# Seven-product (2x2 block) form for the u and output products of a gating layer, and a new pair order in the MLPs

## The chip, the cores and the metric

One core of one Trainium2 chip runs the whole program. The metric is the device time in microseconds (us) of one execution; the number quoted for a kernel is the median of a few runs.

## The reference, cut to what matters

The trunk has four residual layers over 1024 positions of width 1024: a spatial gating layer, an MLP, an RWKV-7 layer and another MLP. The gating layer and the MLPs are what the change touches.

```python
# gating layer: E = 2048, 16 groups of 128 channels, blocks of 128 positions
z = gelu(rmsnorm(x) @ w_in + b_in)            # 1024x1024 @ 1024x4096
u, v = split(z, 2)                            # 2048 columns each
v = layernorm(v) * ln_g + ln_b                # over the 2048 channels
s = einsum('gij,bnjgc->bnigc', w_s * mask, v) + b_s    # one 128x128 matrix for each group
x = x + (u * s) @ w_out                       # 1024x2048 @ 2048x1024
# MLP, after the gating layer and after the RWKV layer
x = x + square(relu(rmsnorm(x) @ w1)) @ w2    # 1024x1024 @ 1024x4096, 1024x4096 @ 4096x1024
```

## The kernel before, in words

Every fp32 product is done as three matmuls on a high and a low part of each operand (`mm3`, lines 155 to 159: high by high, low by high, high by low). The high part is a cast on ScalarE (ACT), the low part a subtraction on VectorE (DVE); `split` does both. One such matmul of 128 x 128 weights by 512 columns is one row of TensorE (PE).

**MLPs** (`mlp`). Both products of an MLP go by a 2x2 block scheme with seven block products instead of eight. `SIDES` names them: M1 = A11 B11, M2 = A12 B21, M3 = S4 B22, M4 = A22 T4, M5 = S1 T1, M6 = S2 T2, M7 = S3 T3, where the S are sums of blocks of the activations and the T sums of blocks of the weights. The first product ("up") runs over 16 pairs of hidden tiles; a product of a pair is 12 matmuls. `prepare(n)` makes the weights of the n-th product six products ahead: `load_pair` brings 2 x 512 KB of w1, `sums` makes T1 to T4 on GpSimd (POOL), `split` makes high and low part in a ring of six buffers. `evict` takes each PSUM result out, squares it, and forms S1 to S4 of the hidden values; all seven blocks are stored to DRAM (`zd`). `seq` is the order of the products: pair p's products are interleaved with M4 and M3 of pair p-1, and the result tiles (`y_of`) alternate between x0 to x3 and x4 to x7. The second product ("dn") has 28 steps (4 groups by 7 products) of 4 quarters, 12 matmuls each; a unit u is half a step's operands: `load_z` brings the stored blocks, `load_w` the tiles of w2, `prepare_z` and `prepare_w` split them (four operand tiles a unit), and `chain` multiplies and adds the result into the residual tiles `xd`. Unit u+4 is prepared while step n runs, u = 2n and 2n+1. The table `meanwhile` says after which of the last products of up the first loads and preparations of dn are issued; from product -14 on the order on PE, DVE, ACT and SyncE (SP, which issues the DMAs) is the written one (`manual_schedule`). Everywhere else a scheduler sets the order.

**Between the layers** `Spread` (before an MLP) takes each residual tile t, stores it (`xmf`), scales it by its norm (`scale`, into one of two tiles xn, here sn_f) and transposes it on PE (`transpose`, tiles st_f). From tiles 0 to 3 come A22 and S1, from tiles 4 to 7 A11, A12, S2, S3 and S4, all split into high and low. `transpose(t-1)` is called right after `scale(t)`.

**Gating layer** (`sgu`). First v in 8 column blocks c (1536 matmuls of 256 columns), kept in 8 SBUF tiles V, with gelu on ACT and the statistics of the layer norm on DVE. Then 16 groups g: two halves of u with 24 matmuls each (768 in all), gelu into x6 or x7, four mixing matmuls for each half into PSUM (s), a DVE operation for scale and bias (line 896, gt), and the product u*s on DVE (line 901). At every second group the v tile is normalised by eight DVE operations (line 877). Then the output product: 8 blocks c, each of 8 tiles t by 2 halves by 6 matmuls (768 in all), added to x on DVE (line 928); during c = 7, `Spread` runs for each finished tile.

**RWKV** (`rwkv`) ends in an output product `product(c, w, ts, out)` over four blocks c; in the last one, c = 3, `Spread` runs tile by tile.

## Time and profile before

| | us |
|---|---|
| median of 3 runs | 2748.62 (2747.3 to 2748.93) |
| the profiled execution, its own time | 2749.38 |
| its span, first to last instruction | 2747.7 |
| PE busy in the span | 2609.6 (95%) |
| DVE busy | 1885.7 (69%) |
| ACT busy | 968.8 (35%) |
| POOL busy | 624.3 (23%) |

The span is what the trace shows; 1.7 us of the execution lie around it. Times in the trace are counted from the span's start. In stages: v until 208 us, u and mixing until 414, the output product until about 595, the first MLP's up until about 922 and dn until 1249, RWKV until about 2093, the second MLP's up until about 2421 and dn to the end.

### The profile page before, as it was taken

Reading aid. Unit: us, or ns where it says so; the run is one execution under the profiler, and the core shown is the slowest. Engines: PE = TensorE matmul, PEld = TensorE weight load, DVE = VectorE, ACT = ScalarE, POOL = GpSimd, SP = SyncE. Lnnn points to the kernel's source line nnn. Section 1 sums busy time; section 2 is a strip of 40 time slices with the busy share of each in tenths; the row PEclk is TensorE's granted clock in tenths of the full one; section 3 lists DMA queues with packets and bytes.
Section 4 is the critical chain, followed back from the end, with each engine's and each line's share of the span. In section 5 each row is a group of like instructions: output and inputs, shape, how many; then the busy total and the mean of one; then the engine's idle time right before and its main releaser. Section 6 shows DMA issues by size and latency. Waiting matters only on the chain. (4 is left out here: it accounts for less than half of the span.)

```text
span 2747.7 us, 41554 instructions
## 1 busy us (share of the span) xinstructions
PE 2609.6 (95%) x16394; PEld 2206.3 (80%) x16394; DVE 1885.7 (69%) x2957; ACT 968.8 (35%) x1579; POOL 624.3 (23%) x481
## 2 busy tenths in 40 slices
PE   8999999989999999999999999977897999989998
PEld 8998888867888778877677898967776888878887
DVE  6446236787666687786667548999678756677777
ACT  4222111243333333345554332324414333333334
POOL 2000000044333000012465413244424333200002
PEclk9999999999999999999899999989899999999999
DMA  5111112124444744332576864444742444384432
GB/s 174 51 47 48 46 58 81 55 91 154 153 146 146 286 166 161 123 115 80 184 178 166 214 170 117 113 101 96 196 131 93 163 138 158 130 324 150 138 130 92
DMA packets 329076, 368.36 MB, mean 134 GB/s; under 512 B 89288, under 2 KB 241968, under 8 KB 328880
## 3 DMA queue, kind: packets, MB, share of 16 engines
q1 hardware_dynamic: 326672, 359.07, 42.0%
q0 software_dynamic: 2064, 6.36, 0.8%
q8 instruction: 129, 2.11, 0.3%
q14 instruction: 67, 0.55, 0.1%
q10 hardware_dynamic: 144, 0.26, 0.0%
HBM read 252.32 MB, written 113.31 MB: 133 GB/s over the span
## 5 line engine op out<-in xcount | busy, mean ns | idle before, releaser
L77 DVE TENSOR_TENSOR wls<-raw,whs 128x1024 fp32r<-128x1024 f32 x84 | 109.7, 1312 | 163.5 <-ACT whs L76 163.2
L76 ACT CAST whs<-raw 128x1024 fp32r<-128x1024 f32 x88 | 91.4, 1047 | 236.7 <-PE wo L159 73.8
L157 PE MATMUL v<-whs,ht_n 128*128 128x256 f32 x512 | 145.3, 284 | 0.2 <-ACT ht_n L307 0.2
L159 PE MATMUL v<-whs,ht_n 128*128 128x256 f32 x512 | 144.3, 282 | 0.2 <-DVE ht_n L162 0.2
L158 PE MATMUL v<-wls,ht_n 128*128 128x256 f32 x512 | 144.2, 282 | 0.0
L331 DVE TENSOR_TENSOR w1s<-w1r,w1s 128x512 fp32r<-128x512 f32 x96 | 90.6, 945 | 63.6 <-ACT w1s L335 63.6
L159 PE MATMUL dnu<-oph 128*128 128x512 f32 x336 | 132.1, 393 | 0.0
L157 PE MATMUL dnu<-oph 128*128 128x512 f32 x336 | 132.1, 393 | 0.0
L158 PE MATMUL dnu<-oph 128*128 128x512 f32 x336 | 131.5, 391 | 0.0
L331 DVE TENSOR_TENSOR xd<-xd,dnu 128x512 f32<-128x512 f32 x128 | 87.5, 684 | 58.4 <-PE dnu L159 58.2
L631 ACT CAST oph<-w2B 128x1024 fp32r<-128x1024 f32 x72 | 75.5, 1049 | 127.5 <-DVE w2B L331 127.5
L629 ACT CAST oph<-zr 128x1024 fp32r<-128x1024 f32 x72 | 75.4, 1048 | 112.4 <-issue 71.5
L928 DVE TENSOR_TENSOR x<-wo,x 128x512 f32<-128x512 f32 x112 | 75.6, 688 | 42.2 <-PE wo L159 42.1
L157 PE MATMUL p<-xs,whs 128*128 128x512 f32 x256 | 104.4, 408 | 0.1
L159 PE MATMUL upc<-sS_f,w1s 128*128 128x512 f32 x256 | 101.2, 395 | 2.8 <-DVE w1s L331 2.8
L158 PE MATMUL p<-xs,whs 128*128 128x512 f32 x256 | 102.3, 400 | 0.9 <-DVE xs L1025 0.9
L159 PE MATMUL p<-xs,wls 128*128 128x512 f32 x256 | 101.9, 399 | 1.1 <-DVE wls L77 1.1
L158 PE MATMUL upc<-sS_f,w1s 128*128 128x512 f32 x256 | 101.7, 397 | 0.8 <-POOL sS_f L331 0.8
L157 PE MATMUL u<-ht_n,whs 128*128 128x512 f32 x256 | 101.7, 397 | 0.0
L157 PE MATMUL upa<-sS_f,w1s 128*128 128x512 f32 x256 | 101.7, 397 | 0.0
L157 PE MATMUL upc<-sS_f,w1s 128*128 128x512 f32 x256 | 101.3, 396 | 0.3 <-ACT sS_f L363 0.3
L158 PE MATMUL upa<-sS_f,w1s 128*128 128x512 f32 x256 | 101.3, 396 | 0.0
(605 smaller groups left out, 8119.3 us busy)
## 6 DMA issues: line engine op xcount, KB each, us to landing
w1r<-in_ffn_w_dram SPq DMA_DIRECT2D x64, 512.0 KB, 4.1
w2B<-in_ffn_w_dram SPq DMA_DIRECT2D x64, 512.0 KB, 5.5
raw<-in_sgu_w_in_dram SPq DMA_DIRECT2D x32, 512.0 KB, 4.2
raw<-in_rwkv_w_rkv_dram SPq DMA_DIRECT2D x32, 512.0 KB, 4.6
...
```

Of the source, the lines that this page charges most:

```text
L76: nc.scalar.copy(out=wh, in_=raw)
L77: (low or nc.vector).tensor_tensor(out=wl, in0=raw, in1=wh.bitcast(F32), op=ALU.subtract)
L157: nc.tensor.matmul(o, sh, mh, start=first, stop=False, skip_group_check=more)
L158: nc.tensor.matmul(o, sh, ml, start=False, stop=False, skip_group_check=more)
L159: nc.tensor.matmul(o, sl, mh, start=False, stop=last, skip_group_check=more)
L331: eng.tensor_tensor(out=out, in0=x, in1=y, op=op)
L629: nc.scalar.copy(out=four[0], in_=z)
L631: nc.scalar.copy(out=four[2], in_=b)
L928: nc.vector.tensor_tensor(out=xs[t][:, dc], in0=o, in1=(xin[t] if c == 0 else xs[t])[:, dc], op=ALU.add)
```

## The change

The function `mlp` becomes `two_products(i, sides, w1, w2, residual, after_factory, gate=None)`, and the gating layer uses it too, with a `Gate`.

- **Gating, u**: 8 pairs of groups by 7 products by 12 matmuls. S1 to S4 of the layer's input are made during v's blocks c = 4 to 7 (`sums_of_halves`: 8 POOL operations, 3 casts on ACT and 3 low parts on DVE for each of four slices), S4's split after v.
- **Gating, v**: two SBUF tiles instead of eight; each finished half block goes to DRAM (`vd`, 16 stores). For each pair its v comes back into x4 to x7 in two loads and is normalised there, four operations on DVE and four on ACT. The mixing matrices and biases also go through DRAM and are reloaded for each pair.
- **Gating, output**: dn's code with 14 steps of 48 matmuls. The residual comes from the kernel's input x.
- **All three two-product stages**: one pair at a time, in the order M1, M5, M6, M2, M7, M3, M4; the MLPs still begin with M5 and M4 of pairs 0 and 1. The result tiles are x0 to x3 alone; x4 to x7 are free at the end of up. T3 and T4 are made on POOL with the product that needs them.
- **Up to dn**: a new table `meanwhile`. The loads of x4 to x7 and of units 0 to 3 come after product -14; the w2 loads after -7 and -4.
- **Spread**: three xn tiles; a tile's transposes come `lag` calls of `tick` after its scaling (3 before the first MLP, 5 before the second). In the gating layer it now runs in the last three steps of dn. In RWKV's output, blocks 2 and 3 of tiles 4 to 7 are interleaved, where block 2 stood ahead of block 3.

```diff
     def scale(self, t):
-        x, xn = self.xs[t], self.xns[t % 2]
+        x, xn = self.xs[t], self.xns[t % 3]
...
     def __call__(self, t):
         self.scale(t)
-        if t > 0:
-            self.transpose(t - 1)
-        if t == NT - 1:
-            self.transpose(t)
+        self.wait.append([t, 0])
...
+    def tick(self):
+        for w in self.wait:
+            w[1] += 1
+        if self.wait and self.wait[0][1] >= self.lag:
+            self.transpose(self.wait.pop(0)[0])
...
-    seq = [("M5", 0), ("M4", 0), ("M5", 1), ("M4", 1), ("M1", 0), ("M2", 0), ("M6", 0), ("M7", 0)]
-    for p in range(1, NP):
-        seq += [("M1", p), ("M4", p - 1), ("M2", p), ("M3", p - 1), ("M6", p), ("M5", p), ("M7", p)]
+    seq = [("M5", 0), ("M4", 0), ("M5", 1), ("M4", 1)] if early else []
+    for p in range(NP):
+        seq += [(m, p) for m in ("M1", "M5", "M6", "M2", "M7", "M3", "M4")]
...
-            ys[p] = [xt(4 * (p % 2) + j, f"y{j}{p}_{i}").rearrange("p (e n) -> p e n", e=2) for j in range(4)]
+            ys.extend(xt(j, f"y{j}_{i}").rearrange("p (e n) -> p e n", e=2) for j in range(4))
...
             elif m == "M6":
                 nc.scalar.copy(out=u2, in_=bank("a", p))
+                nc.scalar.copy(out=y2[:, 1], in_=bank("c", p))
+                if gate:
+                    gate.mix(p, "C11", s24[:, 0])
+                    gate.mix(p, "C12", s24[:, 1])
...
-    meanwhile = {
-        -14: [lambda: load_z(0), lambda: load_z(1)],
-        -8: [lambda: load_w(0, ("B11", "B12"))],
-        -7: [lambda: load_z(2), lambda: load_z(3), lambda: load_w(0, ("B22", "B21"))],
-        -6: [lambda: prepare_z(0), lambda: prepare_w(0)],
-        -5: [lambda: load_x(range(4, 8))],
-        -4: [lambda: prepare_z(1), lambda: prepare_w(1)],
-        -1: [lambda: load_w(1, ("B12", "B11")), lambda: load_x(range(4))],
-    }
...
+        meanwhile = {
+            -14: [lambda: load_x(range(4, 8))] + [lambda u=u: load_z(u) for u in range(4)],
+            -7: [lambda: load_w(0, ("B11", "B12"))],
+            -4: [lambda: load_w(0, ("B22", "B21")), lambda: unit(0)],
+            -3: [lambda: unit(1)],
+        }
...
         up(ready, len(seq))
-        for u in (2, 3):
-            prepare_z(u)
-            prepare_w(u)
+        for f in held:
+            f()
+        load_x(range(4))
+        load_w(1, ("B12", "B11"))
+        unit(2)
+        unit(3)
...
+        def mix(self, p, name, th):
+            e, hf = int(name[2]) - 1, 2 - int(name[1])
+            g = 2 * p + e
+            o = pt(f"s{p}{name}").rearrange("p (n i) -> p n i", n=4)
+            for n in range(4):
+                nc.tensor.matmul(o[:, n, :], self.v[p][hf][:, n, e * P : (e + 1) * P], self.ws[:, 0, e],
+                                 start=True, stop=True)
...
-    product(2, wo[2], range(4, NT), xz)
     xs = [xt(t, f"x2_{t}") for t in range(NT)]
     after = after_factory(xs)
-    product(3, wo[3], range(NT), xs)
+    tick.append(after.tick)
+    product(3, wo[3], range(4), xs)
+    for t in range(4, NT):
+        product(2, wo[2], [t], xz)
+        product(3, wo[3], [t], xs)
```

**Where instructions stand now.** First SP's queue at the end of the second MLP's up. zd1_7... <- y are the stores of the last pair, w2B the loads of w2, xd <- xmf the residual tiles, zr <- zd1_0S3 and zd1_1S3 units 6 and 7, the ones for M7, dn's fourth step. Before:

```order
L513 DMA zd1_7S3_18161<-y215_1_20356 128x512
L513 DMA zd1_7A12_18157<-y015_1_20354 128x512
L513 DMA zd1_7S4_18162<-y315_1_20357 128x512
L584 DMA w2B121_1_20488<-in_ffn_w2_dram 128x2x512 x2
L584 DMA w2B111_1_20491<-in_ffn_w2_dram 128x2x512 x2
L674 DMA xd0_1_18167<-xmf1_0_17685 128x1024
L674 DMA xd1_1_18168<-xmf1_1_17686 128x1024
L674 DMA xd2_1_18169<-xmf1_2_17687 128x1024
L674 DMA xd3_1_18170<-xmf1_3_17688 128x1024
L593 DMA zr1_1_20364<-zd1_0S3_18112 128x1024
L593 DMA zr1_1_20364<-zd1_1S3_18119 128x1024
L593 DMA zr0_1_20219<-zd1_0A22_18109 128x1024
```

Now:

```order
L522 DMA zd1_7S3_18246<-y2_1_18302 128x512
L522 DMA zd1_7S4_18247<-y3_1_18303 128x512
L737 DMA xd0_1_20536<-xmf1_0_17730 128x1024
L737 DMA xd1_1_20538<-xmf1_1_17731 128x1024
L737 DMA xd2_1_20540<-xmf1_2_17732 128x1024
L737 DMA xd3_1_20542<-xmf1_3_17733 128x1024
L639 DMA w2B121_1_20544<-in_ffn_w2_dram 128x2x512 x2
L639 DMA w2B111_1_20547<-in_ffn_w2_dram 128x2x512 x2
L645 DMA zr1_1_20277<-zd1_0S3_18197 128x1024
L645 DMA zr1_1_20277<-zd1_1S3_18204 128x1024
L645 DMA zr0_1_20274<-zd1_0A22_18194 128x1024
```

The loads of xd0 to xd3 stand ahead of the w2 loads where they stood behind them; those of xd4 to xd7, which stood among the last pair's stores, have gone some 60 rows up, to product -14, with the first four unit loads.

Second, PE at the join from RWKV to the second MLP: wo23 are matmuls of `product(3)`, st the transposes of `Spread`, upc0 and upd0 the first two products of up. Before:

```order
L159 MATMUL wo23_71_18037<-wsp6_17603,yh11_17402 128x512
L157 MATMUL wo23_71_18037<-wsp7_17606,yh10_17401 128x512
L158 MATMUL wo23_71_18037<-wsp7_17606,yh10_17401 128x512
L159 MATMUL wo23_71_18037<-wsp7_17606,yh11_17402 128x512
L383 MATMUL st40_f1_17943<-ident_76,sn4_f1_17681 128x128 x4
L383 MATMUL st41_f1_17948<-ident_76,sn4_f1_17681 128x128 x4
L157 MATMUL upc0_1_18212<-sS1_f1_17764,w1s0_1_18187 128x512
L157 MATMUL upd0_1_18228<-sA22_f1_17763,w1s1_1_18190 128x512
L158 MATMUL upd0_1_18228<-sA22_f1_17763,w1s1_1_18190 128x512
L158 MATMUL upc0_1_18212<-sS1_f1_17764,w1s0_1_18187 128x512
L159 MATMUL upc0_1_18212<-sS1_f1_17764,w1s0_1_18187 128x512
```

Now:

```order
L160 MATMUL wo22_71_18130<-wsp5wh_17403,yh10_17511 128x512
L161 MATMUL wo22_71_18130<-wsp5wl_17404,yh10_17511 128x512
L377 MATMUL st50_f1_18098<-ident_81,sn5_f1_17728 128x128 x4
L162 MATMUL wo22_71_18130<-wsp5wh_17403,yh11_17512 128x512
L160 MATMUL wo23_70_18138<-wsp6_17713,yh10_17511 128x512
L161 MATMUL wo23_70_18138<-wsp6_17713,yh10_17511 128x512
L162 MATMUL wo23_70_18138<-wsp6_17713,yh11_17512 128x512
L160 MATMUL wo23_70_18138<-wsp7_17716,yh10_17511 128x512
L161 MATMUL wo23_70_18138<-wsp7_17716,yh10_17511 128x512
L162 MATMUL wo23_70_18138<-wsp7_17716,yh11_17512 128x512
L160 MATMUL wo23_71_18146<-wsp6_17713,yh10_17511 128x512
```

The transposes of tile 4 stood behind the last matmul of the output product, and those of tiles 5 to 7 among the first products of up. Now those of tile 4 stand in the block ahead of this piece, those of the first half of tile 5 in it, and blocks 2 (wo22) and 3 (wo23) of tile 7 alternate.

Third, DVE in the gating layer: wls and w1s are low parts of weights, gt and s the mixing, y the result tiles, upb, upa and upc the PSUM results of the products. Before, two groups:

```order
L77 TENSOR_TENSOR wls33_3474<-raw33_3321,whs33_3473 128x1024
L896 SCALAR_TENSOR_TENSOR gt13_3458<-s13_0_3459,sguv_1060,bs1_114 128x512
L896 SCALAR_TENSOR_TENSOR gt13_3458<-s13_1_3466,sguv_1060,bs1_114 128x512
L901 TENSOR_TENSOR v6_1892<-gt13_3458,u13_3405 128x4x128 x2
L77 TENSOR_TENSOR wls34_3556<-raw34_3403,whs34_3555 128x1024
L896 SCALAR_TENSOR_TENSOR gt14_3540<-s14_0_3541,sguv_1060,bs1_114 128x512
L896 SCALAR_TENSOR_TENSOR gt14_3540<-s14_1_3548,sguv_1060,bs1_114 128x512
L901 TENSOR_TENSOR v7_2129<-gt14_3540,u14_3487 128x4x128 x2
```

Now, half of one pair:

```order
L1042 SCALAR_TENSOR_TENSOR y3_2_2557<-s2C11_2971,sguv_1070,ta_2_2495 128x512
L327 TENSOR_TENSOR w1s22_2_2983<-ta_2_2495,w1s22_2_2983 128x512
L1042 SCALAR_TENSOR_TENSOR y3_2_2557<-s2C12_2977,sguv_1070,ta_2_2495 128x512
L327 TENSOR_TENSOR y0_2_2554<-upb2_2_2986,tu_2_2558 128x512
L327 TENSOR_TENSOR w1s23_2_3001<-tb_2_2496,w1s23_2_3001 128x512
L1024 TENSOR_SCALAR vn41_3090<-vn41_3090,ri_v_2452,vnmr_2450 128x256 x2
L327 TENSOR_TENSOR y0_2_2554<-y0_2_2554,y3_2_2557 128x512
L327 TENSOR_TENSOR y1_2_2555<-y1_2_2555,upa2_2_2896 128x512
L327 TENSOR_TENSOR w1s24_2_3034<-w1r31_2_2773,w1s24_2_3034 128x512
L1042 SCALAR_TENSOR_TENSOR y2_2_2556<-s2C22_3018,sguv_1070,ta_2_2495 128x512
L1042 SCALAR_TENSOR_TENSOR y2_2_2556<-s2C21_3024,sguv_1070,ta_2_2495 128x512
L327 TENSOR_TENSOR y1_2_2555<-y1_2_2555,y2_2_2556 128x512
```

Where two groups held two low parts, four mixing operations (line 896) and four products (line 901), with the normalising of v at every second group, a pair now holds seven low parts, four mixing operations (line 1042), four normalisings (line 1024), three subtractions or additions that take a PSUM result out, four products and S1 to S4. The program has 11817 rows on PE before and 11629 now.

## Rows read from the trace of the kernel before

**Rows 1.** Windows: us, length, busy (count) of PE, PEld, DVE, ACT, POOL, clock, DMA share, GB/s.

```profile
208.00:414.30 206.30, 206.30 (x1027) 172.69 (x1025) 84.31 (x152) 43.41 (x55) 0.00 (x0) 1.00 0.18 54
414.30:576.00 161.70, 161.70 (x712) 133.34 (x712) 112.58 (x148) 29.84 (x28) 10.26 (x8) 1.00 0.21 72
...
628.00:916.00 288.00, 288.00 (x1245) 233.40 (x1245) 189.69 (x264) 95.00 (x164) 92.98 (x68) 1.00 0.46 157
```

**Rows 2.** Windows at the four joins and of their half-clock remainders.

```profile
573.00:626.00 53.00, 43.60 (x204) 33.01 (x203) 51.69 (x95) 33.12 (x65) 26.72 (x20) 0.94 0.21 81
609.90:617.30 7.40, 4.60 (x13) 3.57 (x13) 6.94 (x10) 2.75 (x5) 3.31 (x3) 0.54 0.00 0
...
965.20:968.80 3.60, 3.60 (x9) 2.83 (x10) 3.60 (x4) 0.99 (x2) 0.00 (x0) 0.50 0.59 233
...
2069.60:2114.10 44.50, 31.56 (x160) 24.48 (x160) 44.02 (x83) 25.03 (x51) 19.04 (x13) 0.98 0.24 93
2114.10:2122.50 8.40, 6.71 (x18) 4.54 (x19) 4.84 (x8) 3.93 (x7) 6.22 (x5) 0.50 0.02 6
...
2461.80:2467.30 5.50, 5.50 (x13) 4.34 (x14) 5.50 (x7) 2.89 (x4) 0.00 (x0) 0.51 0.51 180
```

**Rows 3.** PE's waits, gating to first MLP (570 to 640): total, times, longest.

```profile
PE st_f L383 <- DVE sA_f L331: 3.2, 2, 2.6
PE upc L159 <- DVE w1s L331: 2.8, 1, 2.8
```

**Rows 4.** PE's waits, RWKV to second MLP (2065 to 2125).

```profile
PE st_f L383 <- DVE sA_f L331: 8.8, 3, 6.4
PE st_f L383 <- DVE sn_f L374: 5.0, 3, 3.0
```

**Rows 5.** PE's waits from up to dn, first MLP (916 to 966), then second (2410 to 2470).

```profile
PE dnu L157 <- DVE xd L331: 9.1, 1, 9.1
PE upa L157 <- ACT u_f L538: 0.7, 1, 0.7
...
PE dnu L157 <- DVE xd L331: 7.3, 1, 7.3
```

**Rows 6.** Timeline of SP and ACT, second MLP, up to dn: start, length, instruction, [idle before].

```profile
2430.10 0.32 SPq L513 DMA_DIRECT2D zd_7S<-y  x1
2432.54 3.35 SPq L584 DMA_DIRECT2D w2B<-in_ffn_w_dram  x4
2437.30 1.76 SPq L674 DMA_DIRECT2D xd<-xmf  x4
2439.17 0.37 SPq L593 DMA_DIRECT2D zr<-zd_0S  x1
...
2449.50 1.05 ACT L629 CAST op6raw<-zr 128x1024 fp32r<-128x1024 f32 x1 [11.43 <-DMA zr<-zd_0S]
```

**Rows 7.** Groups by form, gating's u stage (210 to 414): count, busy us, mean ns, idle before.

```profile
L886 ACT ACTIVATE u<-u,sguv 128x512 f32<-128x512 f32 x32 | 21.9, 685 | 89.9 <-PE u L159 89.9
L896 DVE SCALAR_TENSOR_TENSOR gt<-s,sguv,bs 128x512 f32<-128x512 f32 x30 | 21.2, 744 | 1.0 <-PE s L893 0.9
L877 DVE TENSOR_SCALAR v<-v,ri_v,vnmr 128x256 f32<-128x256 f32 x64 | 21.1, 407 | 0.0
...
L901 DVE TENSOR_TENSOR v<-gt,u 128x512 f32<-128x512 f32 x30 | 19.4, 683 | 0.0
```

**Rows 8.** Groups by form in the first MLP's up (640 to 900).

```profile
L331 DVE TENSOR_TENSOR w1s<-w1r,w1s 128x512 fp32r<-128x512 f32 x41 | 39.1, 954 | 28.8 <-ACT w1s L335 28.8
...
L331 POOL TENSOR_TENSOR te<-tb,w1r 128x512 f32<-128x512 f32 x13 | 20.6, 1587 | 47.8 <-DVE w1s L331 47.8
...
L331 DVE TENSOR_TENSOR w1s<-ta,w1s 128x512 fp32r<-128x512 f32 x14 | 13.9, 992 | 0.0
...
L331 DVE TENSOR_TENSOR w1s<-te,w1s 128x512 fp32r<-128x512 f32 x13 | 8.8, 676 | 0.0
```

**Rows 9.** Groups by form in the first MLP's dn (969 to 1249), DVE.

```profile
L331 DVE TENSOR_TENSOR oph<-zr,oph 128x1024 fp32r<-128x1024 f32 x30 | 36.5, 1218 | 0.2 <-ACT oph L629 0.2
```

More of the change, by code (lines that the diff above doesn't have):

```diff
@@ L172, in trunk, with channel_vectors @@
     nc.gpsimd.memset(zero, 0.0)
-    def channel_vectors(name, parts):
+    def channel_vectors(name, parts, tag):
         n = sum(v.shape[0] // P for v in parts)
-        stage = zt(7, f"{name}_stage")[:, :P]
+        stage = tp.tile([P, HB], F32, tag=tag, name=f"{name}_stage")[:, :P]
         r = 0
@@ L522, in with_q21, with with_q12, finish, rest @@
             store(p, "S3", s13[:, 1])
-        sp0.u[1] = tp.tile([P, HB], F32, tag="td", name=f"u2_{i}")
-        def evict(m, p):
-            u1, u2, u3 = sp0.u
+        def with_q12(p):
+            y1, y2, s13, s24 = ys
+            tt(v, s24[:, 1], s24[:, 0], y1[:, 1], ADD)
+            store(p, "S4", s24[:, 1])
+        held = []
+        def evict(m, p):
+            if not ys:
+                ys.extend(xt(j, f"y{j}_{i}").rearrange("p (e n) -> p e n", e=2) for j in range(4))
+                u12.extend(tp.tile([P, HB], F32, tag=t, name=f"{t}_{i}") for t in ("tu", "td"))
+            y1, y2, s13, s24 = ys
+            u1, u2 = u12
+            todo, held[:] = list(held), []
+            def finish(q, n, e, then=lambda: None):
+                if gate:
+                    if m != "M4":
+                        gate.act(q, q, 2 * p + e)
+                    def rest():
+                        tt(v, q, q, gate.taken.pop(n), MUL)
+                        if n != "C21":
+                            store(p, {"C11": "A11", "C12": "A12", "C22": "A22"}[n], q)
+                        then()
+                    held.append(rest)
+                else:
+                    square(v, q)
+                    if n != "C21":
+                        store(p, {"C11": "A11", "C12": "A12", "C22": "A22"}[n], q)
+                    then()
@@ new lines, in evict @@
+                if gate:
+                    gate.mix(p, "C11", s24[:, 0])
+                    gate.mix(p, "C12", s24[:, 1])
+            elif m == "M2":
+                tt(v, y1[:, 0], bank("b", p), u1, ADD)
+                finish(y1[:, 0], "C11", 0)
+            elif m == "M7":
+                tt(v, y2[:, 1], y2[:, 1], bank("a", p), SUB)
+                if p < early:
+                    nc.scalar.copy(out=y2[:, 0], in_=bank("a", p))
+                    tt(v, y2[:, 0], bank("d", p), y2[:, 0], ADD)
+                    finish(y2[:, 0], "C21", 0)
+                finish(y2[:, 1], "C22", 1)
+                if p < early:
+                    with_q21(p)
+                if gate:
+                    gate.mix(p, "C22", s13[:, 1])
+                    gate.mix(p, "C21", s13[:, 0])
+                    gate.mixing(p + 1)
@@ L552, in evict @@
             elif m == "M3":
-                y1, y2, s13, s24 = y_of(p)
                 tt(v, y1[:, 1], bank("c", p), u2, SUB)
-                square(v, y1[:, 1])
-                store(p, "A12", y1[:, 1])
-                tt(v, s24[:, 1], s24[:, 0], y1[:, 1], ADD)
-                store(p, "S4", s24[:, 1])
+                finish(y1[:, 1], "C12", 1)
+                if p < early:
+                    with_q12(p)
+            elif m == "M4" and p >= early:
+                if gate:
+                    gate.act(y2[:, 0], bank("a", p), 2 * p)
+                    finish(y2[:, 0], "C21", 0, lambda: (with_q21(p), with_q12(p)))
+                else:
+                    nc.scalar.activation(out=y2[:, 0], in_=bank("a", p), func=AF.Relu)
+                    tt(v if p > NP - 3 else g, y2[:, 0], y2[:, 0], y2[:, 0], MUL)
+                    with_q21(p)
+                    with_q12(p)
@@ L562, in mlp @@
+            for f in todo:
+                f()
         order = ("M1", "M5", "M6", "M7", "M4", "M3", "M2")
@@ L589, in load_z, with z_of @@
             gr, m = steps[u // 2]
+            nc.sync.dma_start(out=z_of(u), in_=zd[2 * gr + u % 2, SIDES[m][0]])
+        def z_of(u):
+            if gate and u < 2:
+                if ("x", u) not in zr:
+                    zr["x", u] = xt(4 + u, f"zrx{u}").rearrange("p (e n) -> p e n", e=2)
+                return zr["x", u]
             j = u // 2 % 2
@@ L936, in trunk @@
+        gate = Gate()
+        sides = type("Sides", (), {"side": side})
+        return two_products(
+            2, sides, w_in[:, :E], w_out, lambda t: x_in[t * P : (t + 1) * P, :], after_factory, gate,
+        )
     KAPPA = float(np.exp(-0.5))
```

318 lines of the change are left out of this document (174 added, 144 removed).

## The prediction

> **What bounds the kernel now.** I read the busy times first: PE is at work for 2609.6 us of a span of 2747.7, so the end moves only by fewer or faster matmuls or by less PE idle. The windows by stage come next. In the gating layer's u stage and in its output product PE is busy without a gap at full clock, and so it is in the first MLP's up [rows 1]; there a matmul less is time less. 288.00 us for 1245 recorded matmuls is 0.2313 us each [rows 1], 2.78 us for a product of 12 and 11.1 us for a dn step of 48. The windows at the joins show the other losses [rows 2]. From the gating layer to the first MLP PE is idle for 53.00 - 43.60 = 9.4 us; behind it stand 13 matmuls at clock 0.54 that take 4.60 instead of 13 x 0.2313 = 3.0 us, 1.6 more: 11.0 in all, **join A**. From RWKV to the second MLP 44.50 - 31.56 = 12.9 and 8.40 - 6.71 = 1.7 are idle, and 18 matmuls at clock 0.50 take 6.71 instead of 4.2: 17.1 in all, **join D**. In both DVE has no room: it is busy 51.69 of 53.00 and 44.02 of 44.50 us, and PE's waits end on its norm and transpose work (st_f on sA_f and sn_f) [rows 3, 4]. The half clock, 1.2 instead of 2.4 GHz, follows PE's long waits each time. From up to dn PE waits once for 9.1 us in the first MLP, **join B**, and once for 7.3 us in the second, **join E** [rows 5]; 9 and 13 matmuls at half clock follow, which cost 3.60 - 2.1 = 1.5 and 5.50 - 3.0 = 2.5 us [rows 2]. So B is 10.6 and E 9.8. Their releaser, xd, is a DVE addition, but DVE was itself held up: ACT waited 11.43 us for unit 6's block, which SP issued at 2439.17, behind eight 512 KB loads (w2B x4, xd x4), and which ACT read at 2449.50 [rows 6].
>
> **The change part by part.**
> *u.* 8 pairs x 7 x 12 = 672 matmuls replace 768; the 128 mixing matmuls stay. 96 x 0.2313 = **-22.2**. The stage before holds 768 x 0.2313 = 177.6 of its 206.3 us in u, so the mixing has 28.7, or 3.6 for the 16 matmuls of a pair; a pair on PE is then 84 x 0.2313 + 3.6 = 23.0 us.
> *Output product.* 768 matmuls at 161.70 / 712 = 0.2271 are 174.4 us [rows 1]; 14 steps x 48 = 672 at dn's price, 0.2313, are 155.4: **-19.0**. Should some records of the 712 be missing, it is -22.2.
> *Half sums of the input.* 32 POOL operations at about 1.6 us [rows 8] are 51 us during v's last four blocks, about 100 us long, on an engine that does little there; 12 casts and 12 low parts go onto ACT and DVE. Cover: v's matmuls. Nothing, as long as POOL ends before v does; its price otherwise is in the next term.
> *Start of u.* The normalising of v, S4's split and the first weights must be ready as v ends. M1, M5 and M6 need none of S4 and no mixing: 8.3 us of cover. **+1**; bounds 0 and one unhidden chain, a reload from DRAM (10.3 us from issue to use in rows 6) less half the cover, 6.
> *The gating pairs.* DVE does, for a pair: five low parts at 0.954, one at 0.992, one at 0.676, 6.4 us [rows 8]; four mixing operations at 0.744, four products at 0.683, seven additions or subtractions at the same price (no gating row; the nearest), four normalisings at 0.407: 12.1 us [rows 7]. That is 18.6 of 23.0. ACT has 14 casts, copies and gelus and four normalisings, at most 18 x 0.685 = 12.3 [rows 7]; POOL four sums at 1.587, 6.3 [rows 8]. DMA moves 1 MB of weights, 1 MB of v, 0.25 MB of mixing and 1.75 MB of stores, 4 MB in 23 us or 174 GB/s, where up runs at 157 without PE waiting [rows 1]. So PE stays the bound, with 4.4 us of DVE to spare, but DVE works in order: a mixing operation that writes over a result tile waits for that tile's store of the pair before, and the low parts queued behind it wait too, for which PE waits in turn. A store is issued some 2 us ahead of that need by my count of the rows in DVE's order. **+2** for eight pairs; bounds 0 and 1 us a pair, 8.
> The low parts that run beside POOL's sums take 0.954 and 0.992 us, the one that does not 0.676 [rows 8], so the sums cost DVE time already before. The Trainium skill (SBUF — State Buffer, "Who interferes with whom") says that DVE's second port is POOL's and that the pair is locked while one side uses it; the trace agrees with 954 against 676 ns. Taken at its word, all of POOL's 6.3 us would be added to DVE's 16.9 without contention: 23.2 of 23.0 us, an estimate by that page that would make this term +1.6 in steady state, about what I take.
> *From u to dn in the gating layer.* The first blocks that dn needs are those of pairs 0 to 3, stored long before; the residual comes from the input. The first units are issued at products -6 to -2, later than in the MLPs. **+1.5**; bounds 0 and what is left of an E-like wait with half the loads in the way, 6.
> *Join A.* Before, PE has 96 matmuls of the output's last block beside DVE's norm work, 21.8 us at 0.2271; now it has three dn steps, 33.3: 11.5 more. DVE loses 16 - 12 = 4 additions of 0.68 and gains four low parts of 1.218 [rows 9]: 2.2 more. So 11.0 shrinks by 9.3 to 1.7. In-order work is not packed perfectly; I leave 3: **-8.0**. Bounds: left 0 to 8.
> *Join D.* 48 matmuls of block 2 move into the stretch, 11.1 us for PE, with 8 additions, 5.4 for DVE: 17.1 - 5.7 = 11.4 by that alone. The later transposes also end waits for a tile scaled just before (sn_f 5.0 us) [rows 4]. I leave 7.5, between 11.4 and 3: **-9.6**.
> *Joins B and E.* Up ends at 2461.8 - 7.3 - 3 x 11.1 = 2421.2, so unit 6's block was read 28.3 us after it, and PE went on 12.3 us after that. For PE not to wait it must land by 33.3 - 12.3 = 21 us after up's end. Now xd4 to xd7 and the first four units are issued at product -14, some 39 us before up's end, and clear the queue; behind the last store, some 5 us after up's end, stand xd0 to xd3 and the w2 loads, 4 MB, and then unit 6. At the rate of the run before (issue 2432.54 to reading 2449.50 for the same 4.5 MB, 17 us) that is 22; since xd0 to xd2 need not wait for the last store, 18 to 22. DVE's chain of 12.3 us is unchanged. I leave 1 us each: **-9.6** and **-8.8**; bounds: left 0 to 4 each.
> *MLP up.* 16 pairs each, the same products and DVE work in a new order. When M4 followed M7 at once on the same PSUM bank, PE waited 0.7 us for its copy [rows 5]; now M3 (2.78 us) lies between. 0, both MLPs; at most 0.7 a pair, see the last rival.
> Sum: -22.2 - 19.0 + 1 + 2 + 1.5 - 8.0 - 9.6 - 9.6 - 8.8 = -72.7. Against the profiled execution's own 2749.4 (1.7 us more than its span) that is 2676.7; that run lies 0.8 above the median of 2748.62, so **2676**.
>
> **The rivals.**
> 1. *Unit 6 is as late as before.* The two w2 loads and xd0 to xd3 still stand ahead of it, and the bound of 21 us lies inside my 18 to 22. If the stores of the last pair land late, both waits and the half clock behind them stay: 9.6 + 8.8 = 18.4 back, **2694**. Against: some 4 MB are out of the way. Chance 0.15.
> 2. *The gating pairs stop PE.* Each of the eight loses one product's length, 2.8 us, since a store, a reload or DVE's order comes late, and two of the stops drop the clock at 1.5 each: 22.4 + 3 - 2 = 23.4, **2699**. For: DVE would do 18.6 of 23.0 us against 84.31 of 206.30 now, with three loads and seven stores a pair. Against: the spare 4.4 us, and that up in the MLPs runs without a gap with DVE busy 189.69 of 288.00. Chance 0.13. The half clock stands behind each of the long waits above [rows 2]; the Trainium skill (TensorE: Matmul & The Clock Gate, "HAM oscillation") tells of kernels whose repeated waits bring the clock down over and over. By that, an estimate, all eight stops would be paid at 1.5, 9 us more.
> 3. *A and D stay.* DVE is full in both [rows 2], and later transposes don't take work from it. Then 8.0 + 9.6 - 5.7 = 11.9 comes back at least, **2688**. Chance 0.12.
> 4. *Slower.* One pair at a time, with one set of result tiles, lets every pair of all three stages end in a serial tail: M4, its squaring, S1 to S4, their stores, and only then the next pair's writes into the same tiles. There are 8 + 32 = 40 pairs; from 72.7 / 40 = 1.8 us a pair on, the kernel is slower. A whole product each, 2.8, is 112 us: **2788**. For: the alternating tiles are gone. Against: the next pair's first write comes only after three products, 8.3 us, and the tail is about 5. Chance 0.03.
> That the change does not do what it says is out: PE has 188 rows fewer, near the 192 matmuls that fall away.
>
> **How the numbers follow.** Forecast 0.55, rivals 0.15, 0.13, 0.12, 0.03, and 0.02 for better than all bounds. A change of 0.2%, 5.5 us, is what a measurement can tell here from none. The terms' best ends (start, pairs and joins at nothing, D at 3) give 2676 - 4.5 - 3 - 4.5 - 2 = 2662; the worst of two or three of them at once about 2694, and rivals 1 and 3 or 2 alone reach 2699; with part of another beside it 2706. Range 2660 to 2706, which leaves out rival 4, the worse half of rival 2 and a few mixtures. Faster 0.95, same 0.02, slower 0.03.
>
> **What would show it.** In the profile after: u and mixing in about 185 us from v's end, and dn of the gating layer at 11.1 us a step; no wait over 1 us of a product on w1s or on the mixing there (else rival 2, and the releaser says which). At B and E no wait of 7 us on xd, and ACT's wait for unit 6 ending by 21 us after up's end (else rival 1). At A about 3 us idle, at D about 7, without a longer stretch at half clock (else rival 3). Both MLPs' ups as long as before to within 2 us (else rival 4). If PE's busy time falls by less than 38 us, the first two terms are wrong.

## The result, and the profile after

The changed kernel takes **2707.85 us** (2702.72 to 2708.94, 4 runs) where the kernel before takes 2748.71 beside it: a ratio of 0.9849, interval 0.9832 to 0.9866. It is faster by 41 us, not by 73, and lies 2 us above the range. The profiled execution (2702.72 us, span 2701.0) lies 5 us under its median: RWKV up to its output product was 7 us shorter there than in the kernel before, an amount that none of the other kernels below repeats (717.5 to 721.0 us there, 720.2 before). That is most of why the stages in the table add up to 46.7 us and the medians differ by 41.

From the page of the changed kernel, busy time first:

```profile
PE 2563.8 (95%) x16202; PEld 2169.5 (80%) x16202; DVE 1978.6 (73%) x3011; ACT 1051.8 (39%) x1725; POOL 718.2 (27%) x545
```

PE works 45.8 us less (the prediction asked for 38 or more), DVE 93, ACT 83 and POOL 94 us more. The table gives the lengths of the stages between PE's first and last matmuls of each, in the two profiled executions.

| stage | before | after | change | forecast |
|---|---|---|---|---|
| v | 208.2 | 226.1 | **+17.9** | 0 |
| u and mixing | 206.4 | 189.1 | -17.3 | -19.2 |
| output product, joins, first up | 508.6 | 496.1 | **-12.5** | -25.5 |
| first dn (join B) | 325.7 | 315.5 | -10.2 | -9.6 |
| RWKV up to its output product | 720.2 | 712.8 | -7.4 | 0 |
| its output product, join D, second up | 452.5 | 440.5 | -12.0 | -9.6 |
| second dn (join E), end | 326.1 | 320.7 | -5.4 | -8.8 |

Two stages hold the whole miss: v, where nothing was to be lost, and the stretch from the gating layer's u to the first MLP's up.

**v.** A window of the kernel before, then three of the changed one (columns as in [rows 1]):

```profile
125.00:150.00 25.00, 25.00 (x217) 25.00 (x216) 9.85 (x20) 5.62 (x12) 0.00 (x0) 1.00 0.15 43
...
100.00:125.00 25.00, 20.90 (x167) 19.53 (x166) 9.97 (x17) 6.70 (x12) 9.03 (x7) 1.00 0.42 141
125.00:150.00 25.00, 21.33 (x166) 20.95 (x166) 19.19 (x30) 5.92 (x11) 23.12 (x17) 0.93 0.26 81
150.00:175.00 25.00, 18.21 (x139) 18.01 (x140) 12.99 (x23) 7.39 (x14) 8.71 (x7) 0.86 0.30 99
```

A window of 25 us without a gap holds 217 matmuls; the changed kernel's second and third hold 166 and 139, with PE idle for 3.7 and 6.8 us and the clock at half for a part of both (0.93 and 0.86). What the engines waited for from 60 to 226 us (total, times, longest), PE, ACT and DVE:

```profile
PE v L160 <- DVE v L855: 9.4, 3, 6.7
PE rwkvv_ps L189 <- issue: 4.1, 1, 4.1
...
ACT sS L896 <- POOL tas L327: 22.1, 8, 6.1
...
DVE sS L327 <- ACT sS L896: 13.7, 4, 4.9
```

Read from below: DVE waits for ACT's cast of a half sum, ACT for POOL's sum, and PE for DVE's bias addition on v, which frees PSUM. (The transpose of RWKV's constants, rwkvv_ps, has no releaser that the view shows; without the sums, in no_sums below, its wait is gone too.) DVE's timeline (start, length, instruction, [idle before]) shows why the addition is late:

```profile
149.68 0.40 DVE L855 TENSOR_TENSOR v<-v,vb 128x256 f32<-128x256 f32 x1
154.94 1.21 DVE L327 TENSOR_TENSOR sS<-tas,sS 128x512 fp32r<-128x512 f32 x1 [4.86 <-ACT sS L896]
...
156.41 1.41 DVE L327 TENSOR_TENSOR sS<-tas,sS 128x512 fp32r<-128x512 f32 x1
157.95 1.54 DVE L327 TENSOR_TENSOR sS<-tbs,sS 128x512 fp32r<-128x512 f32 x1
159.41 0.41 DVE L855 TENSOR_TENSOR v<-v,vb 128x256 f32<-128x256 f32 x1
```

The additions at 149.68 and 159.41 are of neighbouring tiles; before, such a pair is 2.8 us apart (24 matmuls of 256 columns). The order in which DVE's rows stand in the built program shows the same without a time, here for the slice before (v4 is block 4, v4_3 and v4_4 the PSUM results of its tiles 3 and 4, tas2 and tbs2 slice 2):

```
L327 TENSOR_TENSOR sS11_1417<-tas2_1954,sS10_1416 128x512
L855 TENSOR_TENSOR v4_1414<-v4_3_1546,vb1_112 128x256
L327 TENSOR_TENSOR sS35_1421<-tas2_1954,sS34_1420 128x512
L327 TENSOR_TENSOR sS23_1419<-tbs2_1955,sS22_1418 128x512
L863 BN_STATS vstat<-v4_1414 128x6
L855 TENSOR_TENSOR v4_1414<-v4_4_1575,vb1_112 128x256
L327 TENSOR_TENSOR sS11_1417<-tas3_2198,sS10_1416 128x512
```

The scheduler placed the low parts of all four slices among the tiles of one block, v4 (ahead of tile 0 to ahead of tile 5), although the four calls stand in blocks 4 to 7. That block gives PE 22 us of work; POOL needs 10 to 12 us a slice.

**From u to the first up.** PE's waits from 226 to 640 us:

```profile
PE st_f L377 <- DVE xd L327: 5.6, 1, 5.6
PE dnu L160 <- DVE xd L327: 5.6, 1, 5.6
PE st_f L377 <- DVE sn_f L368: 2.6, 1, 2.6
PE upb L160 <- DVE y L1042: 2.5, 2, 2.3
PE st_f L377 <- DVE sr_f L327: 1.7, 3, 0.6
```

The second row is a wait at the start of the gating layer's dn, of the kind of B and E [rows 5]; the first, third and fifth are join A, still 10.6 us with one of 0.7. At dn, as at E before, ACT comes late to unit 6's block. SP and ACT:

```profile
420.05 3.50 SPq L522 DMA_DIRECT2D zd_3S<-y  x4
427.78 2.94 SPq L737 DMA_DIRECT2D xd<-in_x_dram  x4
430.77 2.04 SPq L639 DMA_DIRECT2D w2B<-in_sgu_w_out_dram  x4
432.91 0.83 SPq L645 DMA_DIRECT2D zr<-zd_0S  x1
...
443.25 1.05 ACT L691 CAST op6raw<-zr 128x1024 fp32r<-128x1024 f32 x1 [7.56 <-DMA zr<-zd_0S]
```

u ended at 415.25, so the block is read 28 us later, where the prediction had asked of B and E that it be 21. In the second MLP it is 2403.51 - 2380.28 = 23 us, and PE waits less:

```profile
2403.51 1.05 ACT L691 CAST op6raw<-zr 128x1024 fp32r<-128x1024 f32 x1 [5.43 <-DMA zr<-zd_0S]
...
2415.76 0.47 PE L160 MATMUL dnu<-op6wh,op6raw 128*128 128x512 f32 x1 [2.65 <-DVE xd L327]
```

### The profile page after: what moved, and what is told of

It reads as the page before. It is cut to its first block, busy times and chain, and to the rows that moved or that the text cites. A ratio compares the mean times of both kernels' runs of the same rounds, so it can differ in the third digit from the quotient of the medians.

```text
span 2701.0 us, 41792 instructions
## 1 busy us (share of the span) xinstructions
PE 2563.8 (95%) x16202; PEld 2169.5 (80%) x16202; DVE 1978.6 (73%) x3011; ACT 1051.8 (39%) x1725; POOL 718.2 (27%) x545
## 5 line engine op out<-in xcount | busy, mean ns | idle before, releaser
L327 DVE TENSOR_TENSOR w1s<-w1r,w1s 128x512 fp32r<-128x512 f32 x120 | 129.0, 1076 | 72.0 <-ACT w1s L331 71.7
L160 PE MATMUL dnu<-oph 128*128 128x512 f32 x416 | 164.2, 395 | 0.0
L161 PE MATMUL dnu<-oph 128*128 128x512 f32 x416 | 163.4, 393 | 0.9 <-DVE oph L327 0.9
L162 PE MATMUL dnu<-oph 128*128 128x512 f32 x416 | 163.7, 394 | 0.0
L327 POOL TENSOR_TENSOR ta<-w1r 128x512 f32<-128x512 f32 x40 | 57.1, 1428 | 394.4 <-DMA w1r<-in_ffn_w_dram 300.9
L331 ACT CAST w1s<-w1r 128x512 fp32r<-128x512 f32 x120 | 74.1, 618 | 123.4 <-PE upa L162 61.5
L327 DVE TENSOR_TENSOR oph<-w2B,oph 128x1024 fp32r<-128x1024 f32 x90 | 109.7, 1219 | 0.0
L327 DVE TENSOR_TENSOR oph<-zr,oph 128x1024 fp32r<-128x1024 f32 x89 | 108.5, 1219 | 0.6 <-ACT oph L691 0.6
L160 PEld LDWEIGHTS v<-whs,ht_n 128*128 128x128 f32 x512 | 98.0, 191 | 11.3 <-DVE v L855 10.0
L331 ACT CAST w1s<-tb 128x512 fp32r<-128x512 f32 x78 | 48.3, 620 | 144.5 <-PE upb L162 67.7
L162 PE MATMUL upc<-sS_f,w1s 128*128 128x512 f32 x256 | 101.5, 397 | 1.1 <-DVE w1s L327 1.1
L327 DVE TENSOR_TENSOR y<-y,y 128x512 f32<-128x512 f32 x152 | 100.1, 683 | 2.3 <-ACT y L1049 1.0
```

Source lines behind the costliest of these rows:

```text
L160: nc.tensor.matmul(o, sh, mh, start=first, stop=False, skip_group_check=more)
L161: nc.tensor.matmul(o, sh, ml, start=False, stop=False, skip_group_check=more)
L162: nc.tensor.matmul(o, sl, mh, start=False, stop=last, skip_group_check=more)
L327: eng.tensor_tensor(out=out, in0=x, in1=y, op=op)
L331: nc.scalar.copy(out=dst[:, 0], in_=x)
```

## The experiments

In each diff, lines of the changed kernel are cut to the edit.

### v: the amount of the sums, or their place

**no_sums**

```diff
+            side["S1"], side["S2"], side["S3"] = side["A22"], side["A11"], side["A21"]
...
+            side["S4"] = side["A12"]
```

> The kernel after without the half sums of the gating layer's input: S1 to S4 are simply the blocks A22, A11, A21 and A12, so POOL, ACT and DVE have none of that work in v's blocks 4 to 7, and the products of u are computed from the wrong sums. Theory (the sums' casts and low parts stand in ACT's and DVE's queues among v's additions, and wait there for POOL): v ends at 208 to 210 us instead of 226, PE waits on 'DVE v' (9.4 us) and on rwkvv_ps (4.1 us) vanish with the stretch at a clock of 0.86 to 0.93, and the time falls by 16 to 20 us. Rival (v is longer because of its stores and the two V tiles, which this kernel keeps): v still ends at 220 or later, the time falls by under 6.

The sums, their casts and low parts and S4's split are left out. 2688.05 us, 0.9778 (0.9755 to 0.9801); v is 207.1 and PE's waits in it are gone. So the half sums cost 19 us.

**manual_sums**

```diff
+        with tc.manual_schedule(engines={ET.PE, ET.DVE, ET.Activation, ET.SP}):
+            for c in range(4, 8):
+                w = stream.get(2, ahead=False)
+                v_open(c)
...
+                splits = sums_of_halves(c - 4)
+                for t in range(NT):
+                    v_product(c, t, w)
+                    v_gelu(c, t)
...
+                    if t == 5:
+                        splits()
```

> The kernel after, with v's blocks 4 to 7 in a written order: POOL's eight sums of a slice at a block's start, their casts and low parts after the block's sixth tile, one slice a block. All the work stays. Theory (order, not amount): v ends at 208 to 211 us and the time falls by 15 to 19 us, nearly as without the sums. Rival (the amount of work on POOL's shared port or on DVE): v ends at 215 or later, since every low part still runs beside POOL; the time falls by less than 11.

2695.9 us, 0.9808 (0.9789 to 0.9826). v is 207.5 with every sum still there. Blocks 4 to 7 stand in the written order now, with the casts and low parts of a slice behind tile 5 of their own block. A window of it:

```profile
150.00:175.00 25.00, 25.00 (x217) 25.00 (x216) 12.57 (x24) 7.74 (x16) 9.31 (x7) 1.00 0.26 85
```

The loss in v is order, not amount. The whole time falls by 12 us only, where 15 to 19 had been expected: some came back at the first pair, whose copy on ACT now stands behind v's norm:

```profile
PE upa L160 <- ACT tu L568: 3.4, 1, 3.4
```

**poolsplit_w2late**: the same casts and low parts on POOL, which then releases nobody in ACT's and DVE's queues (and w2_late's edit, below).

```diff
-                nc.scalar.copy(out=sh[:, k], in_=x)
-                tt(v, sl[:, k], x, sh[:, k].bitcast(F32), ALU.subtract)
+                g.tensor_copy(out=sh[:, k], in_=x)
+                tt(g, sl[:, k], x, sh[:, k].bitcast(F32), ALU.subtract)
```

> The kernel after with casts and low parts of S1, S2 and S3 of the gating layer's input on POOL too, the scheduler's order kept, and the w2 loads of group 1 behind units 6 and 7. Theory (v is held up because ACT and DVE wait in order for POOL): v ends at 207 to 210 us, as with the written order, although the four slices still run one behind the other beside v; POOL's chain of 56 operations at 1.3 to 1.5 us ends by 200. Waits on xd at 5.6, 0.6 and 2.7 us go as in w2_late. Together 20 to 27 us less than the kernel after. Rival (POOL's port use itself slows DVE's additions): v ends at 214 or later.

2693.69 us, 0.9803 (0.9787 to 0.9819), but v is 224.6: the theory missed, and the rival, whose number this is (214 or later), has the wrong cause. PE waits once for 13.0 us, and this time through SP's queue (a row of SP's waits from 140 to 192 us, then SP's and ACT's timeline):

```profile
SPq L1032 <- POOL sS L327: 44.5, 1, 44.5
...
175.97 0.32 SPq L1032 DMA_DIRECT2D ta<-wsd  x1
...
176.82 0.42 SPq L59 DMA_DIRECT2D raw<-in_sgu_w_in_dram  x1
...
182.34 1.04 ACT L76 CAST whs<-raw 128x1024 fp32r<-128x1024 f32 x1 [20.61 <-DMA raw<-in_sgu_w_in_dram]
```

The load of v's next weights (raw) stands behind a load into tile ta, for which SP waits 44.5 us until POOL's last low part out of that tile is done. One in-order queue was freed and another took its place.

### The start of dn: what stands ahead of unit 6

**w2_late**

```diff
         load_x(range(4))
-            load_w(1, ("B12", "B11"))
         unit(2)
         unit(3)
+            load_w(1, ("B12", "B11"))
```

> The kernel after with the w2 loads of group 1 (2 MB) issued behind units 6 and 7 instead of ahead, in all three two-product stages. Theory (unit 6 is late because 4 MB stand ahead of it): PE's waits on xd early in dn go from 5.6, 0.6 and 2.7 us to under 1 each, with the half clock behind them; the time falls by 8 to 13. Rival (DVE's work before the fourth step is the bound, the load only the last releaser): the waits fall by less than half, the time by under 5.

2701.21 us, 0.9825 (0.981 to 0.9841). The waits of 5.6, 0.6 and 2.7 us at the three dn become 0.8 and two that the view no longer lists; the stretch from u to the first up shrinks from 496.1 to 488.3, the second dn (to its last matmul) from 311.2 to 306.7. The whole time falls by 6.6 us, where 8 to 13 had been expected. From 226 to 640 us:

```profile
PE dnu L160 <- DVE xd L327: 0.8, 1, 0.8
```

**before_w2late**: the same move in the kernel before, which had these loads at product -1.

```diff
-            -1: [lambda: load_w(1, ("B12", "B11")), lambda: load_x(range(4))],
+            -1: [lambda: load_x(range(4))],
```

> The kernel before with one move: the w2 loads of group 1 (2 MB) behind units 2 and 3 instead of among up's last products. Theory (unit 6's block is late because of what stands ahead of it in SP's queue): PE's waits on xd, 9.1 and 7.3 us, fall by 4 to 7 each with part of the half clock, the time by 9 to 16. Rival (the loads of xd4 to xd7 and the last stores hold it, which only the new table takes away): the waits fall by less than 2 each.

2742.45 us, 0.9983 (0.9972 to 0.9995). The waits of [rows 5] fall by 3.2 and 3.3 us, between the theory's 4 to 7 and the rival's less than 2:

```profile
PE dnu L157 <- DVE xd L331: 5.9, 1, 5.9
...
PE dnu L157 <- DVE xd L331: 4.0, 1, 4.0
```

In the kernel before the w2 loads were a part of the queue; in the changed one, with the earlier loads of xd4 to xd7 out of the way, they were nearly all that was left.

### Join A: order, DVE's amount, or POOL

**lag5**: the first `Spread`'s transposes five ticks late instead of three. With three tiles xn a tile's normalised values are overwritten before they are transposed, so the first MLP's input is changed.

```diff
-    sgu(n0, x0, load_x, spread_factory("f0", a["norm_ffn_g"][0], 3))
+    sgu(n0, x0, load_x, spread_factory("f0", a["norm_ffn_g"][0], 5))
```

> The kernel after with a lag of 5 instead of 3 calls for the first Spread (gating to first MLP). Theory (PE's 5.6 us wait at the first transposes is one of order: they stand on PE ahead of matmuls that could run, and need a PSUM bank whose eviction stands on DVE behind three scalings): the wait and the half clock behind it go, the first MLP's up ends 6 to 9 us earlier, the time falls by 6 to 9. Rival (DVE's total work is the bound of this join): the wait comes back at later transposes, idle in the join stays within 2 us of now, the time within 3.

2712.5 us, 0.9874 (0.9853 to 0.9894); the join's idle stays at about 10, and the wait comes back at later transposes, as the rival had it. Its longest wait, 4.9 us, is on a scaling into the overwritten tile, so it is a poor test of order, and it gains nothing.

**pool6**: low parts of the next MLP's first six weight products from DVE to POOL.

```diff
-            split(made[m, p], x, v)
+            split(made[m, p], x, g if early and n < 6 else v)
```

> The kernel after with the low parts of the first six weight operands of each MLP's up made on POOL instead of DVE: 6 x 0.68 = 4.1 us less for DVE around each join into an MLP. Theory (DVE's amount of work bounds the join from the gating layer to the first MLP): PE's idle there, 10.6 us now, falls by 3 to 5, the 5.6 us wait of the first transposes to about 2, and the half clock behind it goes; the time falls by 3 to 6. Rival (the order of instructions bounds it): the 5.6 us wait stays within 1 us, the time within 2; POOL's own 1.4 us an operation may cost PE a wait on w1s instead.

2710.99 us, 0.9864 (0.9845 to 0.9883). The wait at A is 5.4 instead of 5.6, and D now has one of 7.2 (10.1 us idle instead of 7.4). Taking 4.1 us of low parts off DVE brings nothing, then, if POOL has to do them. What PE waits for, the rows of the changed kernel at A show, SP, POOL, ACT, DVE and PE in turn:

```profile
533.55 2.10 SPq L441 DMA_DIRECT2D w1r<-in_ffn_w_dram  x4
...
539.53 1.32 POOL L327 TENSOR_TENSOR ta<-w1r 128x512 f32<-128x512 f32 x1 [162.40 <-DMA w1r<-in_ffn_w_dram]
...
546.53 1.28 POOL L327 TENSOR_TENSOR ta<-w1r 128x512 f32<-128x512 f32 x1
...
547.84 0.62 ACT L331 CAST w1s<-ta 128x512 fp32r<-128x512 f32 x1 [8.12 <-POOL ta L327]
...
539.75 2.18 DVE L327 TENSOR_TENSOR opz<-zr,opz 128x1024 fp32r<-128x1024 f32 x1
...
548.50 0.69 DVE L327 TENSOR_TENSOR w1s<-ta,w1s 128x512 fp32r<-128x512 f32 x1 [4.32 <-ACT w1s L331]
...
565.77 0.68 DVE L327 TENSOR_TENSOR xd<-xd,dnv 128x512 f32<-128x512 f32 x1
...
566.51 1.11 PE L377 MATMUL st_f<-ident,sn_f 128*128 128x128 f32 x4 [5.64 <-DVE xd L327]
```

ACT's cast of a weight sum waits 8.12 us for POOL's fifth sum; behind it stand the casts of the last dn operands, so DVE idles 4.32 us, then does their low parts, the additions and three scalings, and only then (565.77) empties the PSUM tile that PE's transposes need. And the rows of DVE beside POOL are long: 2.18 where [rows 9] have 1.218. POOL itself had stood idle for 162.40 us until the w1 loads landed, which SP issued at 533.55; no run issues them earlier, so whether that alone would cure the join is open.

**pool_weights**: the first four weight products cast and halved on POOL, so ACT no longer waits.

```diff
+            if early and n < 4:
+                g.tensor_copy(out=made[m, p][:, 0], in_=x)
+                tt(g, made[m, p][:, 1], x, made[m, p][:, 0].bitcast(F32), SUB)
+            else:
+                split(made[m, p], x, v)
```

> The kernel after with casts and low parts of the first four weight operands of each MLP's up (those made from POOL's sums) on POOL instead of ACT and DVE. In the kernel after, the cast of the third of them stands in ACT's queue ahead of the casts for dn's last step in the gating layer, and ACT waits 8.1 us there for POOL's fifth sum; DVE then waits 4.3 us for ACT, and the additions and scalings behind it come late. Theory (this one row makes the join lose): ACT's 8.1 us wait is gone, PE's 5.6 us wait at the first transposes falls to under 2, the join's idle from 10.6 to 5 to 7, the time falls by 4 to 8. Rival (PE's transposes only wait on the norm's own chain and the PSUM bank): the wait stays above 4 us. POOL's longer queue may cost the join into the second MLP 1 to 3 us.

2714.88 us, 0.9873 (0.9859 to 0.9886). ACT's wait is gone, but PE's stays at 5.0 and the idle of A at 11.1. D has a wait of 8.3 now, and 10.4 us idle instead of 7.4. DVE in its trace:

```profile
546.99 2.32 DVE L327 TENSOR_TENSOR oph<-zr,oph 128x1024 fp32r<-128x1024 f32 x1
...
550.96 1.77 DVE L327 TENSOR_TENSOR w1s<-w1r,w1s 128x512 fp32r<-128x512 f32 x1
...
553.26 3.67 DVE L327 TENSOR_TENSOR w1s<-tb,w1s 128x512 fp32r<-128x512 f32 x1
```

The time that ACT's wait had cost, DVE now loses beside POOL.

**act6, nosum01 and act6_nosum01** set POOL's sums against DVE's amount: act6 takes six low parts off DVE (a second cast on ACT stands in for them, the first piece of the diff), nosum01 takes away POOL's eight sums for pairs 0 and 1 (the second piece).

```diff
+            if early and n < 6 and i == 0:
+                nc.scalar.copy(out=made[m, p][:, 0], in_=x)
+                nc.scalar.copy(out=made[m, p][:, 1], in_=x)
...
+            if early and p < 2 and i == 0:
+                b.update(T1=b["B11"], T2=b["B22"], T3=b["B12"], T4=b["B21"])
```

> The kernel after; in the first MLP the low parts of up's first six weight operands are not computed: ACT casts the same operand a second time in their place (6 x 0.62 us more for ACT, 6 x 0.68 = 4.1 us less for DVE, nothing for POOL). Theory (DVE's amount bounds the join): the join's idle falls from 10.6 by 3 to 4, the 5.6 us wait to about 2. Rival (order): the wait stays within 1 us.

> The kernel after; in the first MLP the sums T1 to T4 of pairs 0 and 1 are not made, the products take B11, B22, B12 and B21 in their place. POOL's eight sums around the join are gone, and with them ACT's 8.1 us wait for the fifth, and DVE's slow operations beside them (1.7 to 2.3 us in place of 1.2). Theory (POOL's sums make DVE late): the idle falls to 4 to 7, the 5.6 us wait to under 3. Rival (order): the wait stays within 1 us.

> Both of the last two: no sums for pairs 0 and 1 and no low parts for the first six weight operands of the first MLP. If DVE's amount of work, with what POOL adds to it, bounds the join, its idle falls to 4 or less and the half clock behind it goes; if the order does, PE still waits over 4 us at the first transposes, with DVE idle before them.

act6: 2715.98 us, 0.9888 (0.9856 to 0.992); the wait is 6.1 and the join's idle 13.6. nosum01: 2703.45 us, 0.9842 (0.9812 to 0.9873); from u to the first up 489.7 instead of 496.1. Both together: 2704.46 us, 0.9846 (0.9818 to 0.9875), and 489.1, with 5.4 us idle at the transposes. The gain shows in the stretch; the whole times, 0.9842 and 0.9846, can't be told from the changed kernel's 0.9849. PE's waits in nosum01, 226 to 640 us:

```profile
PE dnu L160 <- DVE xd L327: 6.4, 1, 6.4
PE st_f L377 <- DVE sn_f L368: 2.2, 1, 2.2
...
PE st_f L377 <- DVE sr_f L327: 1.1, 2, 0.6
...
PE st_f L377 <- DVE rm_n L244: 0.6, 1, 0.6
```

Join A is 3.9 us, near the 3 of the forecast; the first row is the start of dn, which the edit doesn't touch. With the sums gone, 4.1 us less on DVE change the stretch by 0.6 us (ACT has 3.7 us more to do in both act6 runs, so DVE's amount is not tested quite alone). So POOL's sums for the next MLP's first pairs hold the join up, in two ways: as a releaser in ACT's queue, and by slowing DVE's rows beside them. How the loss divides between the two stays open, since taking away the first alone (pool_weights) put more of the second in its place.

### Join D: the lag, or the interleaved blocks

**lag3_second**

```diff
-    rwkv(box["n1"], xs, spread_factory("f1", a["norm_ffn_g"][1], 5))
+    rwkv(box["n1"], xs, spread_factory("f1", a["norm_ffn_g"][1], 3))
```

> The kernel after with a lag of 3 instead of 5 calls for the second Spread (RWKV to second MLP); the third xn tile and the interleaved blocks stay. Theory (the later transposes are what ended PE's waits for a tile scaled just before): PE's idle in this join, 7 us now, rises by 3 to 6. Rival (the interleaved blocks, 11 us more of PE work in the stretch, did it alone): idle stays within 1.5 us.

2714.25 us, 0.9872 (0.9854 to 0.989). The join's idle is about 10 us against 7.4, a rise between the theory's 3 to 6 and the rival's 1.5; the second up is 1 us longer. Of the 12.0 us that the stretch gained, the longer lag gives some 3 (443.7 against 440.5). No run tests the interleaved blocks or the third tile alone, so the rest is not divided; and the whole time can't be told from the changed kernel's.

### The gains together

**manual_w2late** has the edits of manual_sums and w2_late.

> v's blocks 4 to 7 in written order and the w2 loads of group 1 behind units 6 and 7. The two gains lie in different stages, so they should add: 2708 - 15 - 8 = 2685 (2681 to 2689). Rival (they overlap): above 2690.

**2681.19 us**, 0.9754 (0.9741 to 0.9767), the fastest of all: 26.7 under the changed kernel, 5 above the prediction's 2676. The two edits alone gave 12.0 and 6.6; each of these differences is uncertain by some 5 us (by the intervals), so that they gain more together is not shown. v is 207.4, the stretch to the first up 489.2, the second dn 306.7. Join A is as it was, and the longest wait that it has left from 100 to 640 us:

```profile
PE st_f L377 <- DVE xd L327: 5.4, 1, 5.4
PE upa L160 <- ACT tu L568: 3.4, 1, 3.4
```

**manual_w2late_poolweights** adds pool_weights.

> Three edits together: v's blocks 4 to 7 in written order, the w2 loads of group 1 behind units 6 and 7, the first four weight operands of each MLP's up wholly on POOL. By the terms so far, from 2708: -15 (v, net of the 3.4 us at the first pair), -8 (up to dn), -4 to -8 (join): 2677 to 2683. Rival (as the low parts alone on POOL showed, the join into the second MLP pays it back): 2684 or more, and no faster than without the third edit.

2690.43 us, 0.9786 (0.9773 to 0.98): the rival's number. D's wait of 8.2 us comes with it, and 12.6 us are idle at A instead of 9.6. With pool6's edit instead of it, the time is 2683.9 (0.9767, 0.9746 to 0.9787). That run had been expected at 2682 (2677 to 2688), with 3 to 5 us from POOL; join A kept its wait of 5.6 there, so the hit is luck. Neither move to POOL pays.

## Why the prediction was wrong, point by point

- **What bounds the kernel**: right. PE is the bound, and the time went where PE idles or runs at half clock.
- **u, -22.2, and the gating pairs, +2**: right. The stage has -17.3 against -19.2, with 3.5 us idle in it: 1.0 in the first pair, 2.3 in the second, and no gap over 0.2 in the other six, so rival 2, a stop in every pair, is out. DVE works 136.0 of the 189.1 us, 17.0 a pair where 18.6 were forecast. The 2.3 us are the stop that the prediction described, once instead of eight times: a mixing operation waits for the store out of the tile that it writes over. DVE's timeline:

```profile
262.29 0.75 DVE L1042 SCALAR_TENSOR_TENSOR y<-s1C,sguv,ta 128x512 f32<-128x512 f32 x1 [3.37 <-DMA zd_0S<-y]
```

- **Half sums of the input, "nothing, as long as POOL ends before v does"**: the step that failed most. POOL ended the sums at 159 us, v ended at 226; the condition was met and the price was 18 us. The cover was counted as amount (51 us of POOL beside 100 us of v), and nothing was asked about the 24 rows on ACT and DVE that wait for POOL, or about what is queued behind them. The order of the built program, which needs no run, shows 12 of them in one block. manual_sums has the same amount and no loss in v.
- **Output product, -19.0**: the measured share is nearer -21: in w2_late 12 us of the 488.3 are waits and half clock, in the kernel before 11 of 508.6, so 497.6 - 476.3. That is close to the other price that the prediction gave, -22.2, for matmul records missing from the trace.
- **From u to dn, +1.5**: mis-sized, with its bound of 6 as well. The wait of 5.6, the 12 matmuls behind it that take 4.5 us instead of 2.8, and 0.9 more make 8.2. "Half the loads in the way" was wrong: eight 512 KB loads stood there (xd x4, w2B x4), as at E before [rows 6]. w2_late takes most of it away.
- **Join A, -8.0**: nothing of it came; 10.6 us idle and some 1.5 of half clock stay, where 11.0 were. The step added up DVE's work against 11.5 us more of PE's, and read PE's waits as norm and transpose work; the 2.8 us on w1s in [rows 3], a weight's low part, it passed over. DVE had the room and stood idle 4.32 us in the middle, behind ACT's cast that waits for POOL's sum. Without POOL's sums (nosum01) the idle is 3.9. Rival 3 forecast the result for A, but for another reason (DVE full).
- **Join D, -9.6**: -12.0 over output product and up together, but the hit is in part luck. At the join itself 7.4 us are idle, and 11 matmuls at half clock follow, about 2.2 us (4.7 - 11 x 0.2313): 9.6 in all, where 7.5 were forecast to be left of 17.1. So the join gave 7.5; the other 4.5 lie elsewhere in the stretch, and no run shows what brought them. PE's rows with idle before them, and the stretch at half clock:

```profile
2058.34 1.23 PE L377 MATMUL st_f<-ident,sn_f 128*128 128x128 f32 x8 [1.39 <-DVE s_f L327]
2065.20 0.50 PE L160 MATMUL upd<-sA_f,w1s 128*128 128x512 f32 x1 [2.26 <-ACT w1s L331]
2067.82 0.91 PE L377 MATMUL st_f<-ident,sn_f 128*128 128x128 f32 x4 [2.12 <-DVE s_f L327]
2070.27 0.79 PE L162 MATMUL upc<-sS_f,w1s 128*128 128x512 f32 x1 [1.12 <-DVE w1s L327]
...
2070.00:2075.00 5.00, 4.73 (x11) 3.73 (x12) 5.00 (x8) 1.05 (x3) 4.70 (x4) 0.52 0.00 0
```

- **B, -9.6, and E, -8.8**: B right (-10.2, a wait of 0.6). At E the block came 23 us after up's end, just outside the 18 to 22 and past the 21 that the prediction named; 2.65 us of wait and 1.5 of half clock stay, 4.1 where 1 was left. B's 0.6 is a good draw: in the nine other kernels that leave these loads where they are, unit 6's block is read 21.7 to 24.6 us after up's end, and PE waits 1.2 to 2.2 us at B and 1.1 to 4.0 at E. With the w2 loads behind unit 6 the block is read at 17.7 to 18.7 and the waits are gone. The mechanism held, the margin was too small, and rival 1 came true for a part.
- **MLP up, 0**: in neither up does PE stop behind the first products, so rival 4 is out.
- **The range**: by the prediction's own prices rivals 1 and 3 together are 18.4 + 11.9 = 30.3 us, so 2706 and not 2699.

The three terms v (18), join A (9) and start of dn (7) are 34 us; the forecast was short by 32, and the smaller misses nearly cancel. The three have one thing in common: what stands ahead of a row in its queue was not asked, or counted wrongly. At A the slower DVE rows beside POOL are part of it, in a share that stays open.
